# A hybrid encoder block on one core: four paired weight slabs in a row, summed blocks kept in the residual's memory

## The chip, the cores and the metric

The kernel runs on one core of one Trainium2 chip. The metric is the device time of one execution in microseconds (us). TensorE (PE in the profile, with PEld for its weight loads) multiplies, VectorE (DVE) and ScalarE (ACT) work on elements, GpSimd (POOL) and SyncE (SP) mostly issue transfers here. Each engine works through its own list of instructions in the order in which the built program has them; they wait for each other through semaphores.

## The reference

One encoder block over 256 rows of 2048 features, in float32:

```python
h = rms_norm(x, norm_g[0]);  q, k, v, g, lr, u_f, u_h, u_s = split(h @ w_in)
mix = concat(gla(...), fnet(u_f), hyena(u_h), shortconv(u_s))     # three of them normed
x = x + mix @ w_out
x = x + cross_attention(rms_norm(x, norm_g[1]), mem_n, w_xq, w_xkv, w_xo)
gate, up = split(rms_norm(x, norm_g[2]) @ w_gate_up)              # 2048 -> 2 x 5632
x = x + (silu(gate) * up) @ w_down                                # 5632 -> 2048
return rms_norm(x, final_norm_g)
```

The change touches the gate/up product, and through it the beginning of the down product.

## The kernel before, in words

**Weights as a stream.** All weights are laid out on the host as 252 slabs of 128 x 2048 floats (1 MB), in the order in which TensorE uses them. Class `Stream` loads slab after slab on SP's queue into three `raw` buffers. A float32 weight is used as a high part, rounded by a ScalarE cast (`wh`), and a low part, the difference on VectorE (`wl`); the rows are split in the same way, and a product is three matmuls: high x high, high x low, low x high (`part`, L432 to L434). The casts and differences go half a slab at a time (1024 columns) into weight places: three in the pool `wp`, and one more in a pool that is lent for a stage (`st.extra`). `_fill` keeps up to three halves ahead of the one in use.

**Plain and paired slabs.** In gate/up and down a plain slab (N in a plan) holds four row blocks of 128 for 512 columns: 4 x 2 x 3 = 24 matmuls of 512 columns. A paired slab (S) holds two row blocks for two column blocks, and is multiplied with seven products in place of eight, by sums of its blocks and of the rows (`take_sums`, `paired_rows`): 7 x 3 = 21 matmuls, but its parts have to be made: four parts of 1024, 512, 1024 and 1024 columns (`_sums`), and additions of blocks. In gate/up two of the sums come ready from memory: for each paired slab SP loads the fourth block twice into a 128 x 1024 tile `two` (two buffers of a pool `tw`), and a GpSimd transfer adds the second and third block to it on the way (L101, L102). VectorE makes the other two by two additions (L158). The rows' sums (`z`, three tiles of 1024) are made once, in the background, by `combine`.

**The gate/up stage.** `gate_up` first multiplies 512 gate and 512 up columns in eight plain slabs (slabs 120 to 127), and then, ten times, a group of eight slabs with the plan `GROUP = "NNSNSNSN"` (slabs 128 to 207). At the end of a group's paired slabs `mixed` puts their products together, `gated` applies Silu, and at the group's end `upped` makes the hidden rows, turns them on VectorE (L557) and GpSimd stores them to memory (L559, tensor `hidden`).

**The background.** Work that may run beside the stream sits in generators that `poll` steps between matmuls. A planner counts the time of TensorE (`pe`, 0.68 per product of 512 columns) and what VectorE owes (`dve`); it steps the background only where VectorE owes little:

```python
    def dve(self, n, ops=1):
        self.owed += n / 960 + 0.155 * ops
    def poll(self):
        for e in list(self.q):
            if self.owed < OWED and self.now >= e[1]:      # OWED = 0.9
                self.step(e)
```

One of the generators is `fetch`: it loads hidden rows back (GpSimd, L564, into one of eleven tiles `tmp`) and splits them into high and low part (a ScalarE and a VectorE instruction of 128 x 256) for the down product. Rows 0 to 21 are fetched early, within gate/up; `gate_up` ends with `drain(early)`, which steps that generator to its end. Rows 0 to 7 go to `act4` to `act11`, 8 to 21 to `f0` to `f13`, the next ones to the halves of `z`. `down` begins with plain slabs of rows 12, 13, 14 and so on.

After all is written down, a scheduler orders each engine's instructions by its own estimate of times, except where `keep_place` holds an instruction behind the one before it on its engine.

**The residual.** `res`, four tiles of 128 x 1024, holds the block's running x; the down product adds to it. In gate/up nothing reads it.

Of the kernel before, what the change touches and what calls it, by code (L numbers as in the profile page):

```python
# [23 lines left out]
P = 128  # L24
# [3 lines left out]
DFF = 5632  # L28
# [16 lines left out]
GROUP = "NNSNSNSN"  # L45
# [4 lines left out]
PAIRED = {a + i for a, plan in [(GATE_UP + 8 * j, GROUP) for j in range(10)] + [(DOWN, PASSES[0]), (DOWN + 22, PASSES[1])]  # L50
          for i, x in enumerate(plan) if x == "S"}
SUMMED = {i for i in PAIRED if i < DOWN}
# [19 lines left out]
class Stream:  # L72


    def __init__(self, tc, pools, W, bg):
        self.tc, self.nc, self.W, self.bg = tc, tc.nc, W, bg
        self.rawp, self.wp = pools
        self.order = []
        self.n = self.made = 0
        self.after = []  # L80
        self.halves = []
        self.at = self.phase = 0
        self.raw = None
        self.extra = self.sums = None
        self.places = []
        self.two = []

    def _buffers(self, n, m):
# [165 lines left out]
class Block:  # L254
    def __init__(self, ctx, tc, t):
# [11 lines left out]
        self.kept = itertools.count()  # L267
        self.run()
# [194 lines left out]
    def paired_rows(self, w, cols, slots, sums, plan, mixed, first, ready=None, late=0, before=None, swap=False):  # L463
# [23 lines left out]
        for i, kind in enumerate(plan):  # L487
            if before:
                before(i)
            if kind == "S":  # L490
# [76 lines left out]
    def run(self):  # L567
# [21 lines left out]
        self.gk = [nc.dram_tensor(f"state{i}", (R, P), F32, kind="Internal").ap() for i in range(4)]  # L589
        self.vd = nc.dram_tensor("values", (P, 8 * 512), F32, kind="Internal").ap()  # L590
# [18 lines left out]
        with self.tc.tile_pool(name="wx", bufs=1) as st.extra:  # L609
# [257 lines left out]
    def attention(self, ps):  # L867
        tc, nc, act, st = self.tc, self.nc, self.act, self.st
        with tc.tile_pool(name="atp", bufs=1) as atp, tc.tile_pool(name="kp", bufs=1) as kp, \
# [111 lines left out]
            st.extra = None  # L981
# [47 lines left out]
    def mlp(self):  # L1029
        tc, nc, act = self.tc, self.nc, self.act  # L1030
        with tc.tile_pool(name="fp", bufs=1) as fp:
            self.gap(fp, 192)
            f = [fp.tile([P, 512], F32R, name=f"f{i}") for i in range(14)]
            z = [fp.tile([P, 1024], F32R, name=f"z{i}") for i in range(3)]
            f = act[4:12] + f + [z[i // 2][:, i % 2 * 512:i % 2 * 512 + 512] for i in range(6)] + self.h3
            with tc.tile_pool(name="wy", bufs=1) as self.st.extra:
                self.gap(self.st.extra, 64)
                with tc.tile_pool(name="tw", bufs=2) as self.st.sums, tc.tile_pool(name="gp", bufs=1) as gp:
# [8 lines left out]
    def gate_up(self, gp, f, z):  # L1047
# [39 lines left out]
        def fetch(k0, k1, ahead, pause, wait=0):  # L1087

            m = {}
            for k in range(k0, k1 + ahead):  # L1090
# [5 lines left out]
                if k >= k0 + ahead:  # L1096
                    while wait and self.bg.now < stored[(k - ahead) // 4] + wait:
# [20 lines left out]
        def combined():  # L1118
            for ks, z in sums:
# [3 lines left out]
        sums = [((2 * i, 2 * i + 1), z[i]) for i in range(GROUP.count("S"))]  # L1123
        comb = self.bg.add(combined())
        ps = self.gemm_rows("w_gate_up", [0, DFF], self.h3,
                            parts=[(range(8), [0]), (range(8, 12), [0]), (range(12), [1]), (range(12, 16), [0]), (range(12, 16), [1])],
                            before=lambda n: n in (1, 3) and self.bg.drain(self.late if n == 1 else last))
# [5 lines left out]
        for j in range(1, DFF // 512):  # L1133
            upped(j, self.paired_rows("w_gate_up", [j * 512, DFF + j * 512], self.h3, sums, GROUP, mixed, gated, swap=j % 2 == 0)[0])
# [3 lines left out]
    def down(self, f, sp):  # L1138
# [54 lines left out]
        for i, plan in enumerate(PASSES):  # L1193
# [5 lines left out]
            def before(j):  # L1199
                while plan[j] == "S" and len(made) <= plan[:j].count("S"):  # L1200
                    self.bg.step(next(e for e in self.bg.q if e[0] is g))
                if late and j == len(plan) - 2:
                    st.extra = None
# [687 lines left out]
```

## Time and profile before

| | us |
|---|---|
| median of 3 runs | 1437.49 (1437.12 to 1438.29) |
| profiled execution | 1434.72 |
| its span, first to last instruction | 1432.9 |
| TensorE busy | 1423.0 |
| VectorE busy | 1145.7 |
| ScalarE busy | 815.8 |
| GpSimd busy | 234.6 |

The page gives each engine's busy time, then the span in 40 slices of 35.8 us with a digit for the busy tenths, then the chain of work that ended last. A line of a group reads: line of the code, engine, operation, output<-inputs, shapes, count | busy us, mean ns of one | idle us of that engine just before them, and what ended most of it. A line of a timeline reads: start, length, engine, line, operation, tiles, count [idle before <-what ended it]. A stretch lists for each engine its busy us and number of instructions, then TensorE's granted clock, the share of the 16 transfer engines and their GB/s. The granted clock is 1.00 throughout.

### The profile page before, as it was taken

The page shows a single profiled execution, that of the slowest core. Times are in us where ns is not written, and L with a number is a line of the kernel's source. Part 1 is how long each engine was busy: PE and PEld are TensorE (multiplying, and loading weights), DVE is VectorE, ACT ScalarE, POOL GpSimd, SP SyncE. Part 2 cuts the span into 40 slices and gives each one's busy share as a digit, 9 for nine tenths or more (in the row PEclk, how much of TensorE's full clock was granted, in tenths as well). Part 3 has the DMA queues.
Part 4 walks back from the last instruction along what each step waited for, and adds up shares of the span by engine and source line. Part 5 has one row for each costly group of instructions (what it writes and reads, how often), then busy time and mean ns, then how long its engine had stood idle before and what let it go on. Part 6 is the DMA issues. An engine that isn't in the chain of part 4 may idle for free.

```text
span 1432.9 us, 18653 instructions
## 1 busy us (share of the span) xinstructions
PE 1423.0 (99%) x6589; PEld 1181.4 (82%) x6589; DVE 1145.7 (80%) x1738; ACT 815.8 (57%) x1183; POOL 234.6 (16%) x306
## 2 busy tenths in 40 slices
PE   9999999999999999999999999999999999999997
PEld 8888888888888888888888888888888888788886
DVE  6667868777877767777677888889888888989997
ACT  7556565446745555556455556555555556655655
POOL 0000100013212223531430121122011002000000
PEclk9999999999999999999999999999999999999999
DMA  9877554456667787865986989899999887665554
GB/s 350 299 291 247 205 202 166 171 172 224 198 199 232 235 271 246 275 201 171 287 242 207 283 280 289 275 275 285 294 293 289 264 265 227 217 231 180 193 219 147
DMA packets 73038, 343.80 MB, mean 240 GB/s; under 512 B 10957, under 2 KB 12654, under 8 KB 45168
## 3 DMA queue, kind: packets, MB, share of 16 engines
q1 hardware_dynamic: 54848, 288.98, 57.6%
q0 software_dynamic: 17664, 52.97, 15.6%
q8 instruction: 51, 0.84, 0.2%
q10 hardware_dynamic: 432, 0.66, 0.1%
q14 instruction: 43, 0.35, 0.1%
HBM read 322.12 MB, written 20.45 MB: 239 GB/s over the span
## 4 chain that ended last, share of the span: by engine, by line
PE 98%; DVE 1%; DMA 0%; ACT 0%; issue 0%; SPq 0%; ACTq 0%
PE pg L432 22%; PE pg L433 22%; PE pg L434 22%; PE pm L432 7%; PE pm L434 7%; PE pm L433 7%; PE pg L380 4%; PE pg L381 2%; PE pm L1344 1%; PE pm L1022 1%; PE pm L993 1%; PE pm L1753 0%; DMA raw<-in_W 0%; DVE res L282 0%; PE pm L994 0%; PE pm L1518 0%
## 5 line engine op out<-in xcount | busy, mean ns | idle before, releaser
L136 DVE TENSOR_TENSOR wl<-raw,wh 128x1024 fp32r<-128x1024 f32 (+1 forms) x413 | 494.1, 1211 | 167.6 <-ACT wh L135 164.8
L135 ACT CAST wh<-raw 128x1024 fp32r<-128x1024 f32 (+1 forms) x413 | 424.7, 1043 | 282.9 <-PE pg L434 188.3
L432 PE MATMUL pg<-wh,act 128*128 128x512 f32 (+1 forms) x1191 | 465.5, 391 | 0.0
L433 PE MATMUL pg<-wl,act 128*128 128x512 f32 (+1 forms) x1191 | 463.9, 389 | 0.1
L434 PE MATMUL pg<-wh,act 128*128 128x512 f32 (+1 forms) x1191 | 463.8, 390 | 0.0
L432 PEld LDWEIGHTS pg<-wh,act 128*128 128x128 f32 x1191 | 224.0, 188 | 47.9 <-issue 1.5
L434 PEld LDWEIGHTS pg<-wh,act 128*128 128x128 f32 x1191 | 223.9, 188 | 47.5 <-DVE act L282 0.6
L433 PEld LDWEIGHTS pg<-wl,act 128*128 128x128 f32 x1191 | 224.0, 188 | 46.5 <-DVE wl L136 1.2
L147 ACT CAST wh<-raw 128x1024 fp32r<-128x1024 f32 (+1 forms) x150 | 137.4, 921 | 149.6 <-PE pg L434 53.8
L148 DVE TENSOR_TENSOR wl<-raw,wh 128x1024 fp32r<-128x1024 f32 (+1 forms) x150 | 155.9, 1060 | 52.8 <-ACT wh L147 52.6
L433 PE MATMUL pm<-wl,act 128*128 128x512 f32 x309 | 120.3, 389 | 0.1
L432 PE MATMUL pm<-wh,act 128*128 128x512 f32 x309 | 120.2, 389 | 0.0
L434 PE MATMUL pm<-wh,act 128*128 128x512 f32 x309 | 120.2, 389 | 0.0
L380 PE MATMUL pg<-act,wh 128*128 128x512 f32 x256 | 90.5, 395 | 0.0
L381 PE MATMUL pg<-act,wl 128*128 128x256 f32 x256 | 71.8, 280 | 0.0
L433 PEld LDWEIGHTS pm<-wl,act 128*128 128x128 f32 x309 | 58.0, 188 | 12.3 <-DVE wl L136 0.4
L434 PEld LDWEIGHTS pm<-wh,act 128*128 128x128 f32 x309 | 58.0, 188 | 12.1
L432 PEld LDWEIGHTS pm<-wh,act 128*128 128x128 f32 x309 | 58.0, 188 | 12.0
L102 POOL DMA_DIRECT2D two<-in_W x30 | 26.6, 885 | 237.6 <-DMA two<-in_W 106.4
L158 DVE TENSOR_TENSOR raw<-raw 128x512 f32<-128x512 f32 x90 | 61.8, 687 | 1.2
L147 ACT CAST wh<-two 128x1024 fp32r<-128x1024 f32 x30 | 31.5, 1051 | 52.0 <-PE pg L434 27.0
L380 PEld LDWEIGHTS pg<-act,wh 128*128 128x128 f32 x256 | 48.1, 188 | 10.5
(375 smaller groups left out, 1819.3 us busy)
## 6 DMA issues: line engine op xcount, KB each, us to landing
raw<-in_W SPq DMA_DIRECT2D x216, 1024.0 KB, 5.6
raw<-in_W SPq DMA_DIRECT2D x30, 768.0 KB, 6.3
two<-in_W SPq DMA_DIRECT2D x60, 256.0 KB, 4.8
two<-in_W POOLq DMA_DIRECT2D x30, 512.0 KB, 9.0
raw<-in_W SPq DMA_DIRECT2D x11, 512.0 KB, 7.1
hidden<-g POOLq DMA_DIRECT2D x22, 256.0 KB, 3.8
tmp<-hidden POOLq DMA_DIRECT2D x44, 128.0 KB, 6.0
features<-tmp POOLq DMA_DIRECT2D x32, 128.0 KB, 5.2
```

What stands on the lines that cost most here:

```text
L102: nc.gpsimd.dma_start(t, W[:, 512:1536], accum_op=ALU.add)
L135: nc.scalar.copy(wh[:, a:b], r[:, a:b])
L136: nc.vector.tensor_tensor(out=wl[:, a:b], in0=r[:, a:b], in1=wh[:, a:b].bitcast(F32), op=ALU.subtract)
L147: nc.scalar.copy(wh, src)
L148: nc.vector.tensor_tensor(out=wl, in0=src, in1=wh.bitcast(F32), op=ALU.subtract)
L158: nc.vector.tensor_tensor(out=out, in0=a, in1=b, op=ALU.add)
L380: self.nc.tensor.matmul(p[:, :], wh, slot[:, :], start=start, stop=False)
L381: self.nc.tensor.matmul(p[:, 0:R], wl, slot[:, 0:R], start=False, stop=stop)
L432: self.nc.tensor.matmul(p, hi, wh, start=start, stop=False)
L433: self.nc.tensor.matmul(p, hi, wl, start=False, stop=False)
L434: self.nc.tensor.matmul(p, lo, wh, start=False, stop=stop)
L993: nc.tensor.matmul(p[:, :], q[d][:, r * P:(r + 1) * P], kt[d][:, :], start=d == 0, stop=False)
```

## The change

- The plan of the first nine groups becomes `"NNSSSSNN"`, four paired slabs in a row; the tenth is `"NNSSNSNN"`, with three as before. There are four row sums `z`, so `f` has twelve tiles, and the early rows 20 and 21 go to halves of the fourth `z`. That tile is free only in the last group, and `fetch` holds rows 20 and 21 until then.
- A fifth weight place (pool `wz`) takes the room of the pool `tw`. It is lent from the beginning of the stage until the sixth slab of the tenth group; `_fill` then keeps four halves ahead. Places are taken in turn from a ring.
- The summed blocks go into the residual's four tiles. The residual is first written to memory (`residual`, 4 x 512 KB on SP), and read back after the last group.
- The fourth block of a paired slab is loaded once (256 KB on SP, when the slab four earlier is loaded); a ScalarE copy of 128 x 512, held in its place, doubles it when the slab three earlier is loaded; then the GpSimd transfer adds the two other blocks.

```diff
-GROUP = "NNSNSNSN"
+GROUPS = *["NNSSSSNN"] * 9, "NNSSNSNN"
...
+AHEAD = (-4, -3)
+SUMS = [{GATE_UP + 8 * j + i + a: GATE_UP + 8 * j + i for j in range(10) for i, x in enumerate(GROUPS[j % len(GROUPS)]) if x == "S"}
+        for a in AHEAD]
...
     def _buffers(self, n, m):
-        pool = self.extra if self.extra and len(self.halves) % 4 == 3 else self.wp
+        slot = min(self.ring, key=lambda x: x[1])
+        pool, slot[1] = slot[0], len(self.halves)
...
     def _load(self, n):
-        if n // 16 + 1 in SUMMED:
-            W, t = self.W[n // 16 + 1], self.sums.tile([P, 1024], F32, name="two", tag="two")
-            for a in (0, 512):
-                nc.sync.dma_start(t[:, a:a + 512], W[:, 1536:2048])
-            nc.gpsimd.dma_start(t, W[:, 512:1536], accum_op=ALU.add)
-            self.two.append(t)
+        if n // 16 in SUMS[0]:
+            t = self.sums[0]
+            self.sums.append(self.sums.pop(0))
+            nc.sync.dma_start(t[:, 0:512], self.W[SUMS[0][n // 16]][:, 1536:2048])
+            self.begun.append(t)
+        if n // 16 in SUMS[1]:
+            t = self.begun.pop(0)
+            mark = len(nc.cur_bb.bb.instructions)
+            nc.scalar.copy(t[:, 512:1024], t[:, 0:512])
+            self.keep(mark)
+            nc.gpsimd.dma_start(t, self.W[SUMS[1][n // 16]][:, 512:1536], accum_op=ALU.add)
+            self.two.append(t)
...
     def _fill(self):
-        ahead = self.at + 1 + min(3 if self.extra else 2, self.n // 16)
+        ahead = self.at + 1 + min(len(self.ring) - 1, self.n // 16)
...
+    def lend(self, pool):
+        self.ring.append([pool, -1])
+        return pool
+    def back(self, pool):
+        self.ring = [x for x in self.ring if x[0] is not pool]
...
-            f = [fp.tile([P, 512], F32R, name=f"f{i}") for i in range(14)]
-            z = [fp.tile([P, 1024], F32R, name=f"z{i}") for i in range(3)]
+            f = [fp.tile([P, 512], F32R, name=f"f{i}") for i in range(12)]
+            z = [fp.tile([P, 1024], F32R, name=f"z{i}") for i in range(4)]
...
                 if k >= k0 + ahead:
+                    while k0 == 0 and k - ahead >= 20 and "free" not in box:
+                        yield
...
+        whole = [x.rearrange("p k r -> p (k r)") for x in self.res]
+        def before(n):
+            if n == 1:
+                self.st.lend(self.wz)
+                for c, x in enumerate(whole):
+                    nc.sync.dma_start(self.rd[:, c * 1024:(c + 1) * 1024], x)
+                self.st.sums = list(whole)
...
         for j in range(1, DFF // 512):
+            plan = GROUPS[(j - 1) % len(GROUPS)]
+            if j == 10:
+                box["free"] = True
...
+        for c, x in enumerate(whole):
+            nc.sync.dma_start(x, self.rd[:, c * 1024:(c + 1) * 1024])
         self.bg.drain(early)
```

More of the change, by code (lines that the diff above doesn't have):

```diff
@@ L608, in run @@
         nc.scalar.copy(self.identr, self.ident)
-        with self.tc.tile_pool(name="wx", bufs=1) as st.extra:
+        with self.tc.tile_pool(name="wx", bufs=1) as self.wx:
+            st.lend(self.wx)
             self.attention(self.mixers())
@@ L1032, in mlp @@
             self.gap(fp, 192)
-            f = [fp.tile([P, 512], F32R, name=f"f{i}") for i in range(14)]
-            z = [fp.tile([P, 1024], F32R, name=f"z{i}") for i in range(3)]
[L1035 to L1038, printed above, removed]
+            f = [fp.tile([P, 512], F32R, name=f"f{i}") for i in range(12)]
+            z = [fp.tile([P, 1024], F32R, name=f"z{i}") for i in range(4)]
+            f = act[4:12] + f + [z[i // 2][:, i % 2 * 512:i % 2 * 512 + 512] for i in range(8)] + self.h3
+            with tc.tile_pool(name="wy", bufs=1) as self.wy:
+                self.gap(self.wy, 64)
+                self.st.lend(self.wy)
+                with tc.tile_pool(name="wz", bufs=1) as self.wz, tc.tile_pool(name="gp", bufs=1) as gp:
                     self.gate_up(gp, f, z)
```

28 lines of the change are left out of this document (18 added, 10 removed).

## The prediction

> **What bounds the kernel now.** I read the page's engine shares first, then its slices, then the chain that ended last.
>
> ```profile
> PE 1423.0 (99%) x6589; PEld 1181.4 (82%) x6589; DVE 1145.7 (80%) x1738; ACT 815.8 (57%) x1183; POOL 234.6 (16%) x306
> DVE  6667868777877767777677888889888888989997
> DMA  9877554456667787865986989899999887665554
> PE 98%; DVE 1%; DMA 0%; ACT 0%; issue 0%; SPq 0%; ACTq 0%
> L432 PE MATMUL pg<-wh,act 128*128 128x512 f32 (+1 forms) x1191 | 465.5, 391 | 0.0
> ```
>
> TensorE works 99% of the span and is 98% of the chain, with no idle time before its main line: the time is the number of matmuls, and a change gains only by removing some without making TensorE wait. What could make it wait is in the slices of the gate/up stage (about 780 to 1195 us): VectorE and the transfers are eight or nine tenths busy there.
>
> The period of a group of eight slabs comes from the copy of `q1`, once a group; what a group holds comes from the stretches, one with and one without the early fetch of the hidden rows.
>
> ```profile
> L1067 ACT COPY g<-pg x5: 578/579/581, 852.0 to 1183.8; 128x512 f32<-128x512 f32 x5
> core 0: us, PE busy (x) PEld busy (x) DVE busy (x) ACT busy (x) POOL busy (x), PEclk, DMA share, GB/s
> 893.00:934.50 41.50, 41.50 (x185) 34.38 (x184) 36.43 (x44) 23.88 (x30) 7.75 (x9) 1.00 0.91 282
> 1142.00:1183.50 41.50, 41.50 (x184) 34.36 (x183) 35.17 (x40) 23.08 (x26) 3.34 (x4) 1.00 0.83 259
> 1300.00:1340.00 40.00, 40.00 (x178) 33.13 (x177) 39.86 (x62) 23.75 (x33) 0.00 (x0) 1.00 0.54 195
> ```
>
> Five copies, every second group, span eight periods: (1183.8 - 852.0) / 8 = 41.48 us. A group is five plain slabs of 24 matmuls and three paired slabs of 21, so 183, and a matmul costs 41.48 / 183 = 0.2267 us. Plain slab 5.44 us, paired slab 4.76 us. The last row shows VectorE at 39.86 of 40 us with TensorE full: a nearly full VectorE alone does not stop TensorE.
>
> **The change, part by part.**
>
> *Matmuls.* Nine groups get a fourth paired slab: 9 x 3 = 27 matmuls go, 27 x 0.2267 = **-6.1 us**. That is all it can gain.
>
> *VectorE and ScalarE per slab.*
>
> ```profile
> L148 DVE TENSOR_TENSOR wl<-raw,wh 128x1024 fp32r<-128x1024 f32 x59 | 72.1, 1222 | 39.6 <-ACT wh L147 39.5
> L148 DVE TENSOR_TENSOR wl<-raw,wh 128x512 fp32r<-128x512 f32 x29 | 19.8, 683 | 0.0
> L158 DVE TENSOR_TENSOR raw<-raw 128x512 f32<-128x512 f32 x32 | 22.0, 689 | 0.7
> L147 ACT CAST wh<-raw 128x512 fp32r<-128x512 f32 x29 | 18.0, 620 | 17.0 <-PE pg L434 9.3 <-PE pm L434 7.6
> 895.00 3.50 DVE L136 TENSOR_TENSOR wl<-raw,wh 128x1024 fp32r<-128x1024 f32 x3 [0.20 <-ACT wh L135]
> 893.92 2.98 ACT L135 CAST wh<-raw 128x1024 fp32r<-128x1024 f32 x3
> ```
>
> A paired slab is three wide differences, a narrow one and two additions: 3 x 1.22 + 0.68 + 2 x 0.69 = 5.72 us on VectorE; a plain slab is 2 x 1.22 = 2.44. Back to back they overlap: three wide ones take 3.50, so 1.14 each, three casts 2.98, so 0.99 each. With about 0.06 us saved per instruction the swap of a plain slab for a paired one adds (5.72 - 0.36) - (2.44 - 0.12) = 3.0 us. A group without fetch then holds 35.2 + 3.0 = 38.2 of 180 x 0.2267 = 40.8 us. It fits. ScalarE's new copy has no row; the 128x512 cast (0.62) bounds it above and the `q1` copy (0.58) below. 39 of them, beside the casts' growth, bring ScalarE to some 28 of 40.8 us: nothing on the path, if no one waits behind it (below).
>
> The Trainium skill, "VectorE: DVE Perf Modes", section "The DRAIN you can't avoid", says that the next operation does not start until the pipe is empty. By that sentence a group's VectorE work is the plain sum of the durations, about 40.9 us, and VectorE would be full; the three in 3.50 us speak against it here.
>
> *Where the early splits go.* The planner in the code counts 5.73 us for a paired slab, 2.44 for a plain one and 12 x 0.688 = 8.26 for a group's output: 3 x 5.73 + 5 x 2.44 + 8.26 = 37.7 against 61 x 0.68 = 41.5 before, but 4 x 5.73 + 4 x 2.44 + 8.26 = 40.9 against 40.8 after. It polls the background only while VectorE owes it under 0.9 us, and now VectorE always does. The built kernel's instruction order shows the result: of the 22 hidden rows split early, one is split in the first groups, three in the last, and **18 stand behind the last output of the stage**. The second half (`down`) begins with row 12, tile f4. The order at that seam:
>
> ```
> VectorE: 2 adds of the last output (need the last gate/up matmul), 2 products, 2 transposes,
>          splits of rows 4,5,...,12 (nine), rows 13, 14, a weight difference, row 15, ...
> POOL:    2 stores of that output, then 29 loads, row 15 the first
> TensorE: last gate/up matmul, 4 matmuls of row 12 (high half), 2 of row 12 (low half), rows 13, 14, 15 ...
> ```
>
> ```profile
> 905.20 1.28 DVE L282 TENSOR_TENSOR h<-h,pg 128x512 f32<-128x512 f32 x2
> 906.40 1.41 DVE L286 SCALAR_TENSOR_TENSOR h<-h,rc,g 128x512 f32<-128x512 f32 x2
> 907.72 1.30 DVE L557 STREAM_TRANSPOSE g<-h 128x512 f32<-128x512 f32 x2
> 908.94 1.18 DVE L136 TENSOR_TENSOR wl<-raw,wh 128x1024 fp32r<-128x1024 f32 x1
> 1239.12 0.75 DVE L282 TENSOR_TENSOR act<-tmp,act 128x256 fp32r<-128x256 f32 x2
> 908.72 1.58 POOL L559 DMA_DIRECT2D hidden<-g  x2 [9.45 <-DVE g L557]
> 914.97 3.53 POOL L564 DMA_DIRECT2D tmp<-hidden  x4 [4.67 <-issue]
> tmp<-hidden POOLq DMA_DIRECT2D x44, 128.0 KB, 6.0
> ```
>
> From the last gate/up matmul (0): the six output operations take 908.94 - 905.20 = 3.74; a pair of splits 0.75, so 0.35 each in a row, nine 3.15; with 0.2 to start, f4's low half is there at 7.1. TensorE has four matmuls (0.9) before it needs it: 6.2 us of waiting. Row 15: its load stands behind the two stores; the first transpose ends at 0.2 + 2.52 + 0.68 = 3.4, so two issues of 0.79 end at 5.0; 6.0 to land gives 11.0, and the cast of the high half 0.4 more. TensorE, going on at 7.1, wants it after 14 matmuls, at 10.3: 1.1 more, with a little for the low half 1.2. Later rows come every 0.88 us against 1.36 us of matmuls a row. Together **+7.4 us**; ends: 5.5 (no wait for row 15) and 10 (loads landing 2.5 later).
>
> *Four paired slabs in a row.* A slab gives four parts of 6, 3, 6, 6 matmuls, each in one of five weight places, so a part's cast waits for the part five before. Inside the run TensorE needs a slab in 4.76 us, VectorE 5.72 - 0.36 = 5.36 us: VectorE falls back 0.6 us a slab. The build answers by moving instructions past one another; in the group of slabs 136 to 143 (a, b: halves of a plain slab):
>
> ```
> ScalarE: 141.2  q1 copy  142.b  141.3  142.a
> VectorE: 142.b  141.3  142.a
> TensorE: 141.0 141.1 141.2 | 2 of 141.3, 2 of 142.a | 4 of 141.3 | rest of 142.a
> ```
>
> 142.b takes the place that 141.0 frees. From its end: 0.2 (a matmul lasts 0.39 and is followed after 0.227, so its result is 0.16 later), three casts 1.05 + 0.99 + 0.99, so 142.a's high half at 3.2. TensorE has 3 + 6 + 2 matmuls, 2.5 us: it waits 0.7. VectorE's three differences end at 0.2 + 1.05 + 3 x 1.15 = 4.7; TensorE comes to 142.a's low half at 3.2 + 6 x 0.227 = 4.6: 0.1 more. So 0.8 in this order, which two groups have. Worked the same way the other orders give 0.1 (two groups), 1.2 (two), 0.8 (two) and 0.8 (one): 0.2 + 1.6 + 2.4 + 1.6 + 0.8 = **+6.6 us**. Ends: 0 (the lead at the run's start covers it) and 13 (twice as much, when a raw slab is late too).
>
> *Transfers.*
>
> ```profile
> raw<-in_W SPq DMA_DIRECT2D x216, 1024.0 KB, 5.6
> two<-in_W SPq DMA_DIRECT2D x60, 256.0 KB, 4.8
> two<-in_W POOLq DMA_DIRECT2D x30, 512.0 KB, 9.0
> DMA to landing us min/median/max: 6.8/9.0/10.9
> res<-in_xT SPq DMA_DIRECT2D x4, 512.0 KB, 6.6
> 902.38 1.05 ACT L135 CAST wh<-raw 128x1024 fp32r<-128x1024 f32 x1 [4.12 <-DMA raw<-in_W]
> ```
>
> A group's weights were 5 x 1 + 3 x (0.75 + 0.5 + 0.5) = 10.25 MB and become 4 x 1 + 4 x (0.75 + 0.25 + 0.5) = 10.0: no relief, no load. The residual's 2 MB out on SP, early in the stage, stands before raw loads: 6.6 us (row of four such tiles), hidden by four halves of lead (4 x 2.72 us); uncovered it costs up to 2.6 us, since a raw load has two slabs' 10.9 us and would need 6.6 + 6.9. Its return at the end runs beside the wait already counted. Both 0. The accumulating load now waits for ScalarE's copy, in ScalarE's queue behind the second Silu and with POOL's stores behind it: for the second paired slab the copy ends about as the group begins, and VectorE's addition comes two plain slabs and half a paired one later, 10.9 + 2.4 = 13.3, less 0.9 for POOL's issue (3.53 / 4): 12.4 us against 9.0 to 10.9 to land. I take 0; the far end is 10.9 plus two sums close ahead (2 x 0.5 MB at 282 GB/s, 3.7) = 14.6, so 2.2 us a group.
>
> *Sum.* -6.1 + 7.4 + 6.6 = +7.9 on the profiled execution's 1434.7: 1442.6. The median of the runs shown is 2.8 above that execution, so **1445.5 us** beside 1437.5.
>
> **Rivals.**
> - *The sums come late* in every group (last paragraph): up to 9 x 2.2 = 20 more, of which I take 13: 1458. For it: the transfers' 0.91 and the 4.12 us that a cast waits for a slab; against it, that this wait stops no matmul before.
> - *The run's waits are not there*: VectorE enters it with its whole lead and only the seam costs: -6.1 + 7.4 = +1.3, 1438.8. For it: the row at 39.86 of 40.
> - *Faster*: the seam is covered, because TensorE finds row 12 split when it comes there; the price of the seam falls to zero and half the run's waits remain: -6.1 + 3.3 = -2.8 to -6.1, 1433. It decides from nine splits and six operations in less than 3 us, half of what the rows give.
> - *VectorE becomes the bound* (durations do not overlap): 40.9 a group plus the waits for casts, 39.6 us over 28 paired slabs in the first row of the differences, 1.4 each: 40.9 + 5.6 = 46.5 against 41.5, 9 x 5.0 + 7.4 = +52: 1490. The rows of three speak against it.
>
> **How the numbers follow.** The forecast 0.49, sums late 0.18, no waits in the run 0.17, faster 0.09, VectorE full 0.07. 0.2% (2.9 us) is about what a measurement tells from no change: same 0.17, faster 0.09, slower 0.74. The range 1436 to 1464 leaves out the faster case, VectorE full and the worst of the late sums. The forecast's own range is 1439 to 1452.
>
> **What would show it.** 27 matmuls fewer. Right: a gap of 5 to 9 us in TensorE at the end of gate/up, closed by VectorE's splits of f4 and f7; a group period of 41 to 42.5 us by the `q1` copies, not 40.8; hardly a split of `act` or `f` in the middle groups; POOL issuing some 29 loads in a row after the last store. Wrong: a period of 40.8 (no waits in the run), no gap at the seam, waits of ScalarE or VectorE for `res<-in_W` landings (late sums), or idle TensorE where the residual goes out or returns.

## The result, and the profile after

The changed kernel takes **1469.8 us** (median of four runs, 1469.4 to 1471.2) against 1437.3: 2.3% slower (ratio 1.0228, 95% interval 1.0211 to 1.0246). The prediction was 1445.5, with a range to 1464. The direction was right, the size was not: 32.5 us came where 8 were forecast. The profiled execution took 1471.2 us with a span of 1469.4, 36.5 more than the span before, with 27 matmuls fewer; it lies 1.3 us above its median, the one before 2.6 below.

From the page after: the engines' busy time, and the shares of the chain that ended last.

```profile
PE 1436.1 (98%) x6562; PEld 1172.8 (80%) x6562; DVE 1172.7 (80%) x1782; ACT 843.9 (57%) x1242; POOL 241.9 (16%) x315
PE 72%; DVE 10%; issue 7%; DMA 6%; ACT 3%; POOL 1%; SPq 0%; ACTq 0%; POOLq 0%; DVEq 0%
```

The matmuls went as counted (6589 - 6562 = 27). But the chain, which was 98% TensorE, now runs for 28% of the time over VectorE, ScalarE, transfers and issue: TensorE waits. The next rows are the copies of `q1` after, and then two stretches of the gate/up stage, first after, then before (columns as in the prediction's stretches).

```profile
L1093 ACT COPY g<-pm x5: 580/588/589, 810.7 to 1159.1; 128x512 f32<-128x512 f32 x5
L1093 ACT COPY g<-pg x5: 577/587/591, 853.7 to 1203.7; 128x512 f32<-128x512 f32 x5
```

```profile
800.00:1190.00 390.00, 380.29 (x1627) 300.76 (x1626) 340.31 (x397) 232.24 (x279) 51.91 (x61) 1.00 0.85 256
```

```profile
800.00:1190.00 390.00, 390.00 (x1722) 323.00 (x1721) 338.02 (x397) 222.46 (x258) 61.82 (x72) 1.00 0.91 279
```

A group takes (1203.7 - 810.7) / 9 = 43.7 us. It had 183 matmuls in 41.5 us, and has 180, which would be 40.8. In the 390 us, 95 fewer matmuls start (1627 for 1722), 21.5 us at 0.2267. TensorE's busy time falls by 9.7 only, since a matmul counts as busy for 0.39 us and is followed after 0.227.

To see where TensorE waits, I add up, stretch by stretch, what each matmul starts later behind the one before than the 0.227 us of an undisturbed one (spacings up to 0.235 left out). Each kernel's profiled execution is counted in this way; the names are those of the experiments below.

| us | time | 720-775 | 775-800 | groups | seam | next 60 us |
|---|---|---|---|---|---|---|
| before | 1437.3 | 0.0 | 0.0 | 0.0 | 0.0 | 0.9 |
| after | 1469.8 | 5.3 | 2.1 | 22.5 | 8.4 | 4.4 |
| a1_three | 1453.3 | 4.6 | 0.0 | 15.3 | 0.0 | 0.8 |
| a2_two_two | 1476.3 | 5.0 | 0.2 | 31.4 | 8.4 | 4.4 |
| a3_raw | 1461.2 | 5.4 | 4.1 | 11.2 | 7.2 | 5.6 |
| a4_nostore | 1463.0 | 0.0 | 0.4 | 21.0 | 8.2 | 4.2 |
| b1_three_four_places | 1440.2 | 6.1 | 0.0 | 0.0 | 0.0 | 1.1 |
| b2_four_places | 1484.5 | 6.0 | 0.0 | 36.7 | 8.1 | 6.3 |
| b3_early | 1461.9 | 2.7 | 4.2 | 22.2 | 0.0 | 3.6 |
| b4_twice | 1489.2 | 7.6 | 0.0 | 38.8 | 8.2 | 4.5 |
| c1_pin | 1455.6 | 4.0 | 0.6 | 7.7 | 8.1 | 4.5 |
| c2_pin_raw | 1453.2 | 6.1 | 1.2 | 5.6 | 8.0 | 4.6 |
| c4_all | 1443.2 | 0.7 | 1.6 | 9.3 | 0.0 | 3.5 |
| c5_pinned_load | 1440.8 | 1.1 | 1.6 | 6.5 | 0.0 | 3.6 |
| c6_paced | 1443.0 | 0.9 | 1.3 | 8.0 | 0.0 | 4.5 |
| d1_three_pin | 1450.5 | 5.2 | 0.0 | 9.1 | 0.0 | 1.1 |
| d2_before_pin | 1440.4 | 0.0 | 0.0 | 3.4 | 0.0 | 0.9 |

For the changed kernel the waits are 42.7, against 0.9 before: 41.8 more, less 6.1 for the matmuls, 35.7 of the 36.5. The largest part is inside the groups. The kernel before had medians of 1436.4 to 1437.8 in the rounds of these runs, so a difference of about a microsecond between two of them says nothing.

Counting matmuls (24 or 21 to a slab) lays the waits in the groups to slabs. Of after's 22.5 us, 7.4 are at the fourth paired slab of a run and the plain slab behind it. The other 15.1 are 8.5 at the second paired slab, 2.1 at the third, 1.0 at the first and the plain slabs before it, and 3.5 in the tenth group, which has only three paired slabs. The same division for other kernels with four paired slabs in a row:

| us | groups | fourth paired slab, plain one behind it | elsewhere |
|---|---|---|---|
| after | 22.5 | 7.4 | 15.1 |
| a3_raw | 11.2 | 8.1 | 3.1 |
| c1_pin | 7.7 | 7.0 | 0.7 |
| c2_pin_raw | 5.6 | 5.3 | 0.3 |
| c5_pinned_load | 6.5 | 4.6 | 1.9 |

What ends TensorE's idle time after, from 800 to 1190 us (total, times, longest; a wait that a running matmul still covers is not in it), is mostly the low or the high half of a paired slab's weights (L163, L162):

```profile
PE pm L456 <- DVE wl L163: 2.7, 4, 0.8
PE pg L456 <- DVE wl L163: 1.5, 2, 0.8
PE pg L455 <- ACT wh L162: 1.2, 4, 0.6
```

One step further back, who waits for whom in the groups (800 to 1190 us; total, times, longest) is read from the waits of ScalarE and VectorE. Before:

```profile
ACT wh L147 <- PE pg L434: 45.0, 32, 2.1
ACT wh L147 <- PE pm L434: 44.5, 32, 2.1
ACT wh L135 <- DMA raw<-in_W: 32.0, 10, 4.2
ACT wh L147 <- DVE raw L158: 17.9, 9, 2.3
DVE wl L148 <- ACT wh L147: 45.2, 48, 1.6
DVE wl L136 <- ACT wh L135: 6.0, 17, 0.9
```

After:

```profile
ACT wh L150 <- DMA raw<-in_W: 52.4, 17, 8.0
ACT wh L162 <- DVE raw L173: 51.3, 17, 5.5
ACT wh L162 <- PE pg L457: 22.9, 15, 5.6
ACT wh L162 <- PE pm L457: 15.0, 14, 2.7
DVE wl L151 <- ACT wh L150: 28.8, 22, 4.3
DVE wl L163 <- ACT wh L162: 20.1, 21, 1.2
```

VectorE waits as long after (28.8 + 20.1 = 48.9) as before (51.2). The difference is one step back, in what ScalarE's casts wait for. Before, they waited mostly for TensorE to free a weight place (45.0 + 44.5): the conversion was ahead, and its idle time was spare. After, they wait for loads of `raw` and for VectorE's own additions (L173): the conversion is behind, and the same idle time may be part of the chain. Work and waits of VectorE together, 340.3 + 48.9, fill 389 of the 390 us: 38.1 + 5.5 in a group of 43.7. By itself that proves nothing, since before they fill as much (338.0 + 51.2); whether these waits cost time, c1_pin and a3_raw test below.

### The profile page after: what moved, and what is told of

It is laid out like the page before. It is cut to its first block, busy times and chain, and to the rows that moved or that the text cites. A ratio compares the mean times of both kernels' runs of the same rounds, so it can differ in the third digit from the quotient of the medians.

```text
span 1469.4 us, 18625 instructions
## 1 busy us (share of the span) xinstructions
PE 1436.1 (98%) x6562; PEld 1172.8 (80%) x6562; DVE 1172.7 (80%) x1782; ACT 843.9 (57%) x1242; POOL 241.9 (16%) x315
## 4 chain that ended last, share of the span: by engine, by line
PE 72%; DVE 10%; issue 7%; DMA 6%; ACT 3%; POOL 1%; SPq 0%; ACTq 0%; POOLq 0%; DVEq 0%
PE pg L456 17%; PE pg L457 16%; PE pg L455 16%; PE pm L456 4%; PE pm L457 4%; PE pm L455 4%; PE pg L403 4%; DMA raw<-in_W 4%; DVE wl L163 4%; PE pg L404 2%; DVE wl L151 2%; ACT wh L150 2%; DVE raw L173 2%; ACT wh L162 1%; PE pm L1389 1%
## 5 line engine op out<-in xcount | busy, mean ns | idle before, releaser
L455 PE MATMUL pg<-wh,act 128*128 128x512 f32 (+1 forms) x1165 | 454.9, 392 | 5.5 <-ACT wh L150 3.6
L456 PE MATMUL pg<-wl,act 128*128 128x512 f32 (+1 forms) x1165 | 455.4, 391 | 2.4 <-DVE wl L151 2.1
L457 PE MATMUL pg<-wh,act 128*128 128x512 f32 (+1 forms) x1165 | 454.1, 390 | 0.0
L455 PEld LDWEIGHTS pg<-wh,act 128*128 128x128 f32 x1165 | 218.8, 188 | 55.0 <-ACT wh L150 5.5
L457 PEld LDWEIGHTS pg<-wh,act 128*128 128x128 f32 x1165 | 219.1, 188 | 46.3 <-DVE act L305 0.6
L162 ACT CAST wh<-raw 128x1024 fp32r<-128x1024 f32 (+1 forms) x177 | 157.3, 917 | 152.6 <-DVE raw L173 77.3
L163 DVE TENSOR_TENSOR wl<-raw,wh 128x1024 fp32r<-128x1024 f32 (+1 forms) x177 | 181.6, 1057 | 32.9 <-ACT wh L162 32.6
L456 PE MATMUL pm<-wl,act 128*128 128x512 f32 x290 | 113.6, 392 | 1.2 <-DVE wl L151 1.0
L455 PE MATMUL pm<-wh,act 128*128 128x512 f32 x290 | 112.6, 391 | 1.0 <-ACT wh L150 1.0
L457 PE MATMUL pm<-wh,act 128*128 128x512 f32 x290 | 112.8, 389 | 0.0
L117 POOL DMA_DIRECT2D res<-in_W x39 | 34.3, 895 | 317.1 <-ACT res L115 301.6
L173 DVE TENSOR_TENSOR raw<-raw 128x512 f32<-128x512 f32 x99 | 68.3, 690 | 0.6
L456 PEld LDWEIGHTS pm<-wl,act 128*128 128x128 f32 x290 | 54.4, 188 | 14.8 <-DVE wl L151 2.7
L455 PEld LDWEIGHTS pm<-wh,act 128*128 128x128 f32 x290 | 54.3, 188 | 13.7 <-ACT wh L150 2.3
L457 PEld LDWEIGHTS pm<-wh,act 128*128 128x128 f32 x290 | 54.5, 188 | 11.1
L587 POOL DMA_DIRECT2D tmp<-hidden x44 | 38.7, 886 | 62.2 <-DVE act L305 34.0
```

The lines of the kernel that those rows point to most:

```text
L117: nc.gpsimd.dma_start(t, self.W[SUMS[1][n // 16]][:, 512:1536], accum_op=ALU.add)
L162: nc.scalar.copy(wh, src)
L163: nc.vector.tensor_tensor(out=wl, in0=src, in1=wh.bitcast(F32), op=ALU.subtract)
L173: nc.vector.tensor_tensor(out=out, in0=a, in1=b, op=ALU.add)
L455: self.nc.tensor.matmul(p, hi, wh, start=start, stop=False)
L456: self.nc.tensor.matmul(p, hi, wl, start=False, stop=False)
```

## Experiments

**Is it the four in a row?**

a1_three has three paired slabs at the old places; a2_two_two has four, two and two. (The first expectations give 23.3 us for the groups where the table has 22.5.)

```diff
-GROUPS = *["NNSSSSNN"] * 9, "NNSSNSNN"
+GROUPS = ["NNSNSNSN"] * 10
```

> The changed kernel with three paired slabs a group at the places they had before (NNSNSNSN in all ten groups); the five weight places, the residual's memory for the sums and the one load with ScalarE's copy stay. If the lost time belongs to the fourth paired slab in a row (the groups' 23.3 us, the seam's 8.4 and the 4.3 behind it), only what lies around the first half of the gate/up stage is left: 1437.3 + 5.3 (the pause at 734 us) + 2.1 (at 784 us) = 1444 to 1445, and the copies of q1 come every 41.5 us. If the residual's memory, the one load and the copy are what costs in the groups, the period is over 42.5 and the time over 1455.

```diff
-GROUPS = *["NNSSSSNN"] * 9, "NNSSNSNN"
+GROUPS = *["NSSNSSNN"] * 9, "NNSSNSNN"
```

> The changed kernel with the same four paired slabs a group, but two and two (NSSNSSNN in nine groups); the outputs stand where they stood. Theory A (four next to each other use up VectorE's lead): the groups' 23.3 us of waiting fall to 0 to 4, the period from 43.6 to 40.8 to 41.3 us, the time to 1447 to 1451. Theory V (a group's work and waits of VectorE are the bound, wherever the slabs stand): the period stays at 43 to 44, the time at 1466 to 1472. Theory L (the slabs behind the run are loaded late, since the three raw buffers come free late): between these, 1453 to 1463, with casts still waiting for landings of raw. The seam stays in all of them.

Measured: 1453.3 and 1476.3. Neither expectation held. Taking the run apart made the groups worse, 31.4 us of waiting for 22.5, and three slabs at their old places still lose 15.3. So four in a row are not dearer than two and two, and something beside the fourth slab costs too.

**The fifth weight place.** b1 and b2 go back to four places, b1 with three paired slabs, b2 with four.

```diff
             if n == 1:
-                self.st.lend(self.wz)
```

> Three paired slabs a group at their old places (as in a1_three) and no fifth weight place: four, as before; the residual's memory, the one load and ScalarE's copy stay. a1_three lost 15.3 us of TensorE's time inside the groups although no run of four was left. Theory P (with a fifth place each cast and difference of weights is emitted one half earlier, so that in VectorE's queue a difference that waits for its place stands ahead of output work that could go): the groups' waiting falls to under 3 us, the period of the q1 copies from 43.2 to 41.5, the time from 1453.3 to 1439 to 1442 (1437.8 and up to 4.6 for the residual's store). Theory C (the sums in the residual's memory, loaded once and copied by ScalarE, cost it): the period stays above 43, the time at 1450 to 1454.

> The changed kernel without the fifth weight place. Theory V (VectorE is the bound: a group's 38.5 us of work and four times 1.2 us in which it waits for the cast of a paired slab's fourth part, which itself waits for VectorE's second addition, 43.3 in all): the places don't matter, the period stays at 43 to 44.5, the time at 1467 to 1476. Theory P (the fifth place puts the work in a worse order): the period falls by the 1.7 us that a1_three had too much, to about 42, the time to 1453 to 1458.

Measured: 1440.2 (1.0027 of before, 1.0012 to 1.0041), no waiting in the groups, as theory P had it; and 1484.5, with 36.7. b1 clears the new way of making the sums: the residual's memory, one load and ScalarE's copy cost nothing inside groups of three. The fifth place costs 13 us with three slabs and saves 14.6 with four, so both theories of b2's expectation fell: V (places don't matter) and P (a gain). How the fifth place hurts with three shows in VectorE's queue in a1_three:

```profile
949.32 0.68 DVE L305 TENSOR_TENSOR h<-g,pg 128x512 f32<-128x512 f32 x1
952.37 1.23 DVE L151 TENSOR_TENSOR wl<-raw,wh 128x1024 fp32r<-128x1024 f32 x1 [2.37 <-ACT wh L150]
953.51 0.68 DVE L305 TENSOR_TENSOR g<-h,pg 128x512 f32<-128x512 f32 x1
```

A weight difference whose cast waits for a place stands in front of the rest of the group's output: VectorE idles for 2.37 us with that output ready, and then has the rest of it and a paired slab to make without a break.

**Late loads.** a3_raw adds a fourth raw buffer of 1536 columns.

```diff
-        self.raw = self.rawp.tile([P, 2048], F32, name="raw", tag="raw")
+        if n // 16 in SUMMED and (n // 16 - GATE_UP) % 8 == 5:
+            self.raw = self.more.tile([P, 1536], F32, name="raw", tag="raw")
+        else:
+            self.raw = self.rawp.tile([P, 2048], F32, name="raw", tag="raw")
```

> The changed kernel with a fourth raw buffer (1536 columns, for the last paired slab of each run), so that the three slabs behind it are loaded one buffer earlier. Theory L (late loads behind the run empty VectorE's lead): casts wait for raw half as long in the groups (58.5 us in 18 waits before it), the groups' waiting falls from 23.3 to under 10, the time to 1452 to 1458. Theories A and V: the waits inside the run stay, 1465 to 1470.

Measured: 1461.2, 11.2 us of waiting in the groups instead of 22.5. Casts wait 28.4 us for plain slabs' `raw` instead of 52.4 (from 800 to 1190 us; the 58.5 of the expectation is from 780 to 1240). VectorE's waits behind those casts fall from 28.8 to 17.6, while those for paired slabs stay (20.1 after, 22.4 here). Half of the groups' loss goes with a buffer; the time stayed 3 us above the range expected of L: the start of the groups and the stretch behind the seam got worse by 3.2.

**VectorE's order.** In a paired slab the fourth part is cast from the result of the second addition (L173, `raw<-raw`). The built kernel put the third part's difference between the two additions. From the timeline after (VectorE, then ScalarE's cast of that fourth part and what follows it):

```profile
1008.74 1.79 DVE L163 TENSOR_TENSOR wl<-raw,wh 128x1024 fp32r<-128x1024 f32 x2
1010.44 0.69 DVE L173 TENSOR_TENSOR raw<-res,raw 128x512 f32<-128x512 f32 x1
1011.04 1.22 DVE L163 TENSOR_TENSOR wl<-res,wh 128x1024 fp32r<-128x1024 f32 x1
1012.18 0.69 DVE L173 TENSOR_TENSOR raw<-raw 128x512 f32<-128x512 f32 x1
1014.06 2.36 DVE L163 TENSOR_TENSOR wl<-raw,wh 128x1024 fp32r<-128x1024 f32 x2 [1.19 <-ACT wh L162]
...
1012.98 2.51 ACT L162 CAST wh<-raw 128x1024 fp32r<-128x1024 f32 x3 [5.48 <-DVE raw L173]
```

ScalarE has waited 5.48 us for the second addition; then VectorE waits 1.19 us for ScalarE's cast, with nothing else in its queue that it may do. c1_pin makes the second addition first. Nothing else differs in the code. The scheduler, though, orders anew: in the first nine groups TensorE's and ScalarE's lists change as well, TensorE's only from the third paired slab on; in the tenth group TensorE's list is the same.

```diff
         nc.vector.tensor_tensor(out=wl, in0=src, in1=wh.bitcast(F32), op=ALU.subtract)
+        if ph == 2 and summed:
+            self.behind(nc.cur_bb.bb.instructions[-1], self.added)
...
             for out, a, b in ops:
                 nc.vector.tensor_tensor(out=out, in0=a, in1=b, op=ALU.add)
+            self.added = nc.cur_bb.bb.instructions[-1]
...
+    def behind(self, late, early):
+        self.tc.add_manual_dep(late, early.name, mybir.DependencyInfo(
+            mybir.DependencyClass.NoSync, mybir.DependencyReason.DATA), reason="order")
```

> The changed kernel with one thing put in another order: in each paired slab VectorE makes its two additions one behind the other, and the third part's difference behind them (S0, S1, A, B, S2, S3 and not S0, S1, A, S2, B, S3), so that ScalarE casts the fourth part while VectorE makes the third's difference. No work is added or taken away. Theory V (in VectorE's order 38.1 us of work and four waits of 1.2 us for that cast make 42.9 us a group, over the 40.8 of TensorE): up to 4.8 us a group come free, the groups' waiting falls from 22.5 us to under 9, the time to 1448 to 1457. Theory L (late raw loads alone): the casts go on waiting for raw, the time stays at 1464 to 1470.

> The same order of additions together with the fourth raw buffer of a3_raw. If the two causes (VectorE's waits for the cast of the fourth part, late raw loads) hold together, as V and L say, and nothing else is behind them: no waiting in the groups above 3 us, the copies of q1 every 40.8 to 41.1 us, 1447 to 1451, which is the changed kernel without its groups' waits (1469.8 - 22.5). If a third cause is there (transfers, sums): the period stays over 41.5, the time over 1453.

Measured: 1455.6 for c1_pin, 14.2 us less than the changed kernel, in the range of theory V. Its VectorE timeline and waits (800 to 1190 us):

```profile
1006.82 0.68 DVE L175 TENSOR_TENSOR raw<-res,raw 128x512 f32<-128x512 f32 x1
1007.54 0.69 DVE L175 TENSOR_TENSOR raw<-raw 128x512 f32<-128x512 f32 x1
1008.15 1.22 DVE L163 TENSOR_TENSOR wl<-res,wh 128x1024 fp32r<-128x1024 f32 x1
1009.43 2.96 DVE L163 TENSOR_TENSOR wl<-raw,wh 128x1024 fp32r<-128x1024 f32 x3
```

```profile
DVE wl L151 <- ACT wh L150: 27.8, 23, 3.3
DVE wl L163 <- ACT wh L162: 1.3, 3, 0.7
```

The wait ahead of the fourth part's difference is gone (20.1 us to 1.3), and TensorE's waiting in the groups falls from 22.5 to 7.7. The waits at the second paired slab (8.5) and in the tenth group (3.5), where TensorE's order is what it was, are gone entirely, so VectorE's order cost them and not TensorE's other moves. It was VectorE's standing still that cost, not ScalarE's: ScalarE's waits for additions rise, from 51.3 to 70.4. Of TensorE's 7.7 us, 7.0 are at the fourth paired slab and the plain one behind it; VectorE still waits behind plain slabs' loads (27.8). With the raw buffer too (c2_pin_raw, 1453.2) TensorE waits 5.6 us in the groups, more than the 3 expected, and a group takes (1185.3 - 815.8) / 9 = 41.06 us by its copies of `q1`. The two causes overlap (14.8 + 11.3 alone, 16.9 together): each alone takes away most of the same 15.1 us, and neither what stands at the run's end. That each does so by emptying VectorE's lead fits the rows, but was not tried by itself.

The same exchange in a1_three and in the kernel before:

> a1_three (three paired slabs a group at their old places, five weight places) with the two additions one behind the other as in c1_pin. If VectorE's wait for the cast of the fourth part is what a1_three lost by as well (36.5 us in 32 waits): the groups' 15.3 us fall to under 5, the time to 1439 to 1443. If it lost by the fifth place's order on its own (a difference that waits 2.4 us for its place in front of output work): 10 or more of the 15.3 stay, 1448 to 1454.

> The kernel before with the two additions one behind the other. VectorE's waits for casts of paired slabs (45.2 us in 48 waits) should fall under 10 us there too, and the time should stay within 2 us of 1437, since there they cost TensorE nothing: VectorE has 5.5 us to spare in a group of 41.5. A gain of over 3 us would say that before is held by VectorE as well.

Measured: 1450.5, with 9.1 us of the 15.3 left, and 1440.4, 3 us slower than before (1.0029, 1.0014 to 1.0045). The first is close to the second case of its expectation, the second missed both of its numbers. So a1_three's loss is in part this wait and in larger part the fifth place; that the row of 2.37 us above is all of that rest was not tried. In the kernel before, VectorE's waits for paired slabs' casts fall only from 45.2 to 34.5 us, since most of ScalarE's casts there wait for a weight place, and those for plain slabs rise from 6.0 to 18.7. Putting the additions together is no gain by itself: of the kernels tried it pays in those in which VectorE's waits hold up TensorE.

**The seam and the early rows.** b3_early lets the planner split early rows in the groups, whatever VectorE owes.

```diff
-            if self.owed < OWED and self.now >= e[1]:
+            if self.owed < self.limit and self.now >= e[1]:
...
         self.bg.drain(comb)
+        self.bg.limit = 1e9
         for j in range(1, DFF // 512):
...
+        self.bg.limit = OWED
         self.bg.drain(early)
```

> The changed kernel, with the early rows of the hidden layer split inside the groups again: between the first group and the last one the planner polls its background whatever VectorE owes. The seam's waits (8.4 us and 4.4 in the 60 us behind it) should be gone in every theory. Theory V (VectorE is the bound inside the groups): 18 splits of 0.35 to 0.42 us come back there as 6 to 8 us, so that the time is 1463 to 1466. If VectorE has idle time to give, where it waits for casts (5 us a group), they cost nothing there: 1456 to 1458.

Measured: 1461.9, 8.0 less. The seam's 8.4 us are gone, the groups' waiting is the same (22.2). The price is neither of the two expected: the splits fill time in which VectorE waited for casts (48.9 us of waits after, 42.2 here), but 2.1 us more are lost as the first group begins, against 2.6 fewer before it, and most of the 4.4 behind the seam stay.

**One load and a copy.** b4_twice loads the fourth block twice.

```diff
-            nc.sync.dma_start(t[:, 0:512], self.W[SUMS[0][n // 16]][:, 1536:2048])
+            for a in (0, 512):
+                nc.sync.dma_start(t[:, a:a + 512], self.W[SUMS[0][n // 16]][:, 1536:2048])
...
-            nc.scalar.copy(t[:, 512:1024], t[:, 0:512])
```

> The changed kernel with the fourth block loaded twice by SP, as before, and without ScalarE's copy; all else stays. If the copy, waiting in ScalarE's queue for its load, holds up the casts behind it: the groups' waiting falls from 22.5 us by 5 or more, the time to under 1465. If it is covered, as the prediction took it: 1468 to 1471, or slightly slower, for 0.25 MB more in each paired slab (39 x 0.25 MB, under 1 us each at 280 GB/s).

Measured: 1489.2, 19.4 more, which neither case expected. Its casts wait 67.3 us for plain slabs' `raw` (52.4 after), whose loads take 10.1 us to land (5.9 after). So if the copy holds anybody up, it is by less than the second load costs, and with four paired slabs the loads are on the chain. Whether it is the quarter of a megabyte in each paired slab or the second load's place in SP's queue was not tried.

**The residual's store.** a4_nostore has neither the store nor the return.

```diff
-                for c, x in enumerate(whole):
-                    nc.sync.dma_start(self.rd[:, c * 1024:(c + 1) * 1024], x)
...
-        for c, x in enumerate(whole):
-            nc.sync.dma_start(x, self.rd[:, c * 1024:(c + 1) * 1024])
```

> The changed kernel without the residual's store and return: the output lacks the residual of the first three stages, the rest of the work stays. If SP's queue, standing behind the third store, is what makes TensorE pause at 734 us, the pause and the low clock behind it go: 5.3 less, and with the pause at 784 us gone too 7.4 less: 1462 to 1465. If the loads of the sums themselves are what delays the raw loads there, it stays at 1469 to 1470.

Measured: 1463.0, 6.9 less, as expected of the store; the pause at 734 us is gone. In the changed kernel's timeline of SP it is a matter of order, not of bytes, and c4_all below, which keeps the store and moves it, loses 0.7 us there. (The last row is the cast that TensorE waited for.)

```profile
714.43 0.33 SPq L1159 DMA_DIRECT2D residual<-res  x1
720.70 0.33 SPq L110 DMA_DIRECT2D res<-in_W  x1
721.43 0.33 SPq L123 DMA_DIRECT2D raw<-in_W  x1
734.76 1.99 ACT L150 CAST wh<-raw 128x1024 fp32r<-128x1024 f32 x2 [7.29 <-DMA raw<-in_W]
```

The first load of sums into the third residual tile may start only when the tile's store has landed. SP stands still for that until 720.70, and the raw load behind it starts up to 6 us late, beside other traffic. SP's waits from 690 to 800 us have the same:

```profile
SPq L110 <- DMA residual<-res: 8.1, 2, 5.9
```

**All mends together.** c4_all is c2_pin_raw with the early rows of b3_early and with the stores and the sums' loads kept behind raw loads in SP's queue. c5_pinned_load also keeps the fourth raw buffer's load in TensorE's order (it was issued 30 us early). c6_paced spreads the early rows.

```diff
+            for c in ((), (0, 1), (2, 3))[n] if n < 3 else ():
+                mark = self.mark()
+                nc.sync.dma_start(self.rd[:, c * 1024:(c + 1) * 1024], whole[c])
+                self.keep_place(mark)
...
+            mark = len(nc.cur_bb.bb.instructions)
             nc.sync.dma_start(t[:, 0:512], self.W[SUMS[0][n // 16]][:, 1536:2048])
+            self.keep(mark)
```

> c2_pin_raw, with the early rows split inside the groups (as in b3_early) and with the residual's four stores and the first loads of sums standing in SP's queue behind raw loads that are not held up by them. If the terms found so far are the whole: 1437.3 - 6.1 (27 matmuls) and no waits: 1431 to 1434, faster than before by 0.2 to 0.4%. If the early rows find no room in VectorE's queue beside 38.1 us of work (20 splits of 0.35 to 0.42 us): up to 8 more, 1436 to 1441. If the store at the first block costs the same in another place: 5 to 7 more.

```diff
+            mark = len(nc.cur_bb.bb.instructions)
             nc.sync.dma_start(self.raw[:, 0:1536], self.W[n // 16][:, 0:1536])
+            self.keep(mark)
```

> c4_all with one more thing: the loads of the paired slabs stand in SP's queue in the order in which TensorE takes them. In c4_all and c2_pin_raw the load into the fourth raw buffer is issued some 30 us before it is wanted, ahead of the next group's plain slabs, and once a group a cast then waits up to 5.8 us for a plain slab, VectorE 2.7 us behind it. If that is what is left of the groups' waiting: c4_all's 9.3 us there fall to under 3, the copies of q1 come every 40.8 to 41.0 us, and the time is 1433 to 1437, level with before or 0.3% faster. If VectorE's work alone (38.1 us of 40.8, and 20 splits in the first six groups) is what is left: 1441 to 1444.

```diff
-        early = self.bg.add(fetch(0, FT - 22, 3, 2.0, 15))
+        early = self.bg.add(fetch(0, FT - 22, 3, 9.0, 15))
```

> c5_pinned_load, with the early rows spread evenly: two to three splits a group over all the groups, not four a group in the first ones (the planner's pause behind a row is 9 us, was 2). In c5_pinned_load TensorE still waits 6.5 us in the groups, nearly all of it in the first five, which hold the splits, and under 0.7 a group in the later ones. If VectorE's fullness there is what is left (38.1 us of work and four splits of 0.4, 39.7 of 40.8): the groups' waiting falls to 2 to 4, the time from 1440.8 to 1437 to 1439. If it is the start of the stage that is late, whatever is split: 1440 to 1442.

Measured: 1443.2, 1440.8 (1.0025 of before, 1.0015 to 1.0036) and 1443.0. In c4_all the seam is gone and the store costs 0.7 us in place of 6.1. None reached the best case of its expectation. c5_pinned_load comes to 3.5 us above before, 29 below the changed kernel; pacing gains nothing, so a late start or a full VectorE is not told apart by it. Of c5_pinned_load's 6.5 us in the groups, 4.6 are again at the fourth paired slab and the plain one behind it. From c5_pinned_load's stretches:

```profile
800.00:1190.00 390.00, 387.06 (x1693) 316.01 (x1692) 364.25 (x434) 249.66 (x310) 70.64 (x82) 1.00 0.92 276
```

VectorE works 364 of 390 us, 93%, and the 6.1 us that the matmuls gain are eaten by what is left: 6.5 in the groups, 2.7 before them, 3.6 behind. No version beat the kernel before.

## Why the prediction was wrong

- **Matmuls, -6.1: right.** 27 fewer.
- **VectorE, "It fits": this step failed.** The work was right (38.2 us a group forecast, 340.3 / 390 x 43.7 = 38.1 measured). The step compared it with 40.8 and took the 2.6 us between as enough. But VectorE also stands still in its own order, 5.5 us a group: 3.2 behind plain slabs' loads (28.8 in the 390 us) and 2.3 for ScalarE's cast of a paired slab's fourth part (20.1). So TensorE waits at the second and third paired slab and in the tenth group, 15.1 us that the prediction had at nothing. With the second of these waits taken out (c1_pin) 0.7 of them are left, with a fourth raw buffer (a3_raw) 3.1. In the kernel before, VectorE's waits had the same total (51.2 us); one step back most of them were ended by TensorE freeing places, and so they were spare; the prediction read them as spare after the change too.
- **The rival that comes out right by luck.** "VectorE becomes the bound" had waits in its sum, 1.4 us for each paired slab: 38.2 + 5.6 would have been 43.8, against 43.7 measured. But after the change the casts of paired slabs cost VectorE 2.3 a group, not 5.6, and the rest is late loads, which the rival does not have; its work of 40.9 is not there. By the Trainium skill's "VectorE: DVE Perf Modes", section "The DRAIN you can't avoid", the next operation waits for the pipe to empty, but one that is not held starts earlier. The prediction took the first half alone; the trace goes on showing an earlier start (three differences, 1.22 + 1.22 + 0.69 by their own durations, in 2.96 us), so the work did not grow: the waits did it.
- **Four in a row, +6.6 (0 to 13): right where it was worked out, and not the whole.** At the fourth paired slab and the plain one behind it TensorE waits 7.4 us over the nine groups. In the group whose order the prediction shows it is 1.1 (0.8 forecast), at the run's last part and at that plain slab, ended by ScalarE's casts and VectorE's differences as it says. This price stays in a3_raw and c1_pin (8.1 and 7.0). The groups' 22.5 us lie beyond the term's far end because the term has only the end of the run: the 15.1 us elsewhere are those of the step above.
- **Seam, +7.4: right in cause, 1.0 short.** TensorE paused for 1.38 us, made its four matmuls and stood for 4.19 until VectorE's splits of the `f` tiles came:

```profile
1217.20 0.39 PE L457 MATMUL pm<-wh,act 128*128 128x512 f32 x1
1218.81 0.50 PE L455 MATMUL pg<-wh,f 128*128 128x512 f32 x1 [1.22 <-ACT f L313]
1219.62 0.39 PE L456 MATMUL pg<-wl,f 128*128 128x512 f32 x1
1224.04 1.22 PE L457 MATMUL pg<-wh,f 128*128 128x512 f32 x2 [4.03 <-DVE f L305]
1225.06 0.63 PE L455 MATMUL pg<-wh,f 128*128 128x512 f32 x1
1225.49 0.63 PE L456 MATMUL pg<-wl,f 128*128 128x512 f32 x1
```

  TensorE went on 1224.04 - 1217.20 = 6.8 us behind the last gate/up matmul (7.1 forecast). The 1.2 for row 15 did not come; TensorE's low clock (below) took 2.7 in its place. The 4.4 us in the next 60 were not foreseen; they stay in every kernel with four paired slabs, also without the seam, and go with three. Their cause was not settled.
- **Transfers, residual and sums, 0: two of four wrong.** Late sums did not come (the rival at 1458): ScalarE and VectorE hardly wait for `res<-in_W`. The return of the residual costs nothing (1.1 us behind the seam in b1_three_four_places, 0.9 before). The store cost 5.3 us and some of the 2.1 behind it, above its bound of 2.6, because the prediction counted its bytes and not SP's order behind it. And "no relief, no load" was not enough: in the groups late loads are on the chain, as a3_raw and b4_twice show, though the transfers are less busy than before (a share of 0.85, 0.91 before).
- **The sum.** -6.1, +7.4 at the start, +22.5, +8.4 and +3.5 (4.4 less before's 0.9) make 35.7. The forecast lacked 28 of them, 16 in the groups, nearly all of that at the places where it had no wait.

## What to carry to other kernels

An engine's idle time is spare only as long as what ends it is the bound's own release; follow each wait one step back, and ask who ends it once the bound moves. When work is added to an engine with an in-order queue, add its waits on the engine that it hands work to, not its durations alone, and look in the built order for a pair that hands work back and forth. A load queued behind one that must wait for a store to land is late by what the landing still takes (5.9 us here), however few bytes it has.

## What the hardware showed beside it

After a pause TensorE may come back at half speed. The granted clock is the third number from the right in these stretches after: two pauses of 2.4 and 1.2 us at 734, with one matmul between, and what follows; the pause of 4.2 us at the seam, and what follows.

```profile
734.00:737.00 3.00, 0.74 (x4) 0.31 (x2) 1.16 (x2) 2.24 (x3) 0.00 (x0) 1.00 0.48 193
737.00:742.00 5.00, 4.05 (x11) 2.99 (x11) 5.00 (x10) 3.38 (x7) 0.42 (x1) 0.66 0.34 90
1219.50:1224.00 4.50, 0.51 (x3) 0.07 (x1) 4.50 (x13) 1.35 (x2) 3.30 (x5) 0.87 0.41 115
1224.00:1228.00 4.00, 3.96 (x9) 3.14 (x10) 2.33 (x5) 0.81 (x2) 4.00 (x5) 0.50 0.82 157
```

At 0.50 the matmuls start 0.427 us apart, eleven of them at the seam; with the spacings of 0.59 and 0.39 at the two ends 2.7 us are lost, so that the pause of 4.2 us cost 6.9. The pause of 2.0 us at 784 brought none of this, and neither did c1_pin's two of 2.6 and 1.2 us at 735, with one matmul between:

```profile
739.00:744.00 5.00, 4.43 (x19) 3.66 (x20) 5.00 (x10) 3.64 (x8) 1.11 (x2) 1.00 0.48 152
```

The Trainium skill, "TensorE: Matmul & The Clock Gate", section "What's actually happening", has a gate that goes to half the clock after an idle window of about 3.4 us that runs free of the kernel. The rows agree with half, and a free-running window would explain why nearly equal pauses differ, which no run here shows by itself. At 734 us, though, neither pause was as long as that window: 2.4 and 1.2 us, with a matmul between.
